# Hidden activations of a squared-ReLU MLP go through DRAM: the MLP in two phases, five of eight down groups by seven block products, the embedding projection between the phases

## The chip, the cores and the metric

The kernel runs on one core of one Trainium2 chip. A core has TensorE for matmuls (PE in the rows; its weight loads are PEld), VectorE (DVE), ScalarE (ACT) and GpSimd (POOL), and SyncE (SP), which here only issues DMAs; GpSimd issues DMAs as well. Operands lie in the on-chip buffer of 128 partitions, sums of matmuls in PSUM. The metric is the time of one execution on the device, in microseconds (us), as the median of the runs shown.

## The reference, cut to what matters

One decoder layer on 512 tokens with a model width of 2048, all in fp32. A gated linear attention comes first; the change does not touch it. Then:

```python
h = h + mix
h = h + square(relu(rmsnorm(h, norm_mlp) @ w_up)) @ w_down   # 2048 -> 8192 -> 2048
gate = sigmoid(rmsnorm(h, norm_ple) @ w_ple_gate)            # 2048 -> 2048
h = h + gate * (p @ w_ple_proj)                              # p: 512 x 256
return rmsnorm(h, norm_final)
```

## The kernel before, in words

**Products.** Each fp32 product is made of three matmuls in a faster 32-bit format (fp32r): both factors are split into a high and a low part, and hi·hi, hi·lo and lo·hi are added up in PSUM (mm3, L140 to L142). The weights are split on the way in by load_w (L126 to L132): SyncE's queue loads a tile `raw`, ScalarE casts it to `whi`, VectorE subtracts to get `wlo`. The pools have 3 buffers for raw, 4 for whi and 4 for wlo.

**Up products.** The hidden width of 8192 is made in 32 groups of 256 columns (up_group). A group walks in 4 chunks of 512 rows over the model width. Each chunk is cut into two-by-two blocks and multiplied by seven block products in place of eight (Winograd's form): sums of weight blocks T on VectorE (L783 to L786), casts (L793), low parts (L794), and 2 x 7 x 3 = 42 matmuls of 256 columns (L800 to L802). The operands on the token side, sums and differences of the blocks of the normalised h, are made once and stay (XS, XA). At the end of a group VectorE combines the seven sums (L808 to L814), applies ReLU and the rest of the norm's scale r2 (L816), ScalarE squares (L818), and the result is split into Sh and Sl (L821, L822).

**Down products.** The hidden values of two groups are one slice of 512. For each of 16 slices, 8 groups of 256 output columns are made plainly: 4 x 2 x 3 = 24 matmuls of 512 columns (down_group). The residual h passes through DRAM: GpSimd's queue loads two row blocks (L850), VectorE adds the sum of the slice (L859), GpSimd's queue stores them (L865). Only the last slice keeps h on the chip and makes the operands U of the gate from it (gain_split).

**Order.** The program is written so that up chunks of slice c alternate with down groups of slice c-1 (the loop at the end of the MLP); a scheduler then orders each engine's instructions, which run strictly in that order on their engine. The buffers in the pools set how far an engine can be ahead of TensorE.

**After the MLP.** p is transposed and split (PT), and for each of five groups of output columns the gate's product runs (ps_g), then for each of 4 blocks of tokens the embedding's projection (embed, ps_ple), the transposes of h (ps_h), and finish, which joins them.

## Time and profile before

| what | value |
|---|---|
| runs shown | 2389.72, 2767.68, 2387.84 us; median 2389.72 |
| profiled execution | 2387.21 us, its span 2385.4 us |
| mean granted TensorE clock | 0.997 |
| TensorE busy | 2366.7 us, 99% |
| VectorE busy | 1550.7 us, 65% |
| ScalarE busy | 868.2 us, 36% |
| GpSimd busy | 223.0 us, 9% |
| DMA | 382.85 MB, mean 160 GB/s |

Busy time counts the time in which an engine works on an instruction. Matmuls overlap each other, so the mean duration of one is longer than its share of the time; what a matmul costs is read from start to start. The granted clock is given as a share of TensorE's full 2.4 GHz.

### The profile page before, as it was taken

To read this page: it belongs to the slowest core of one execution; us is meant where nothing else is said; L and a number is where in the kernel's file an instruction comes from. 1 tells how busy PE (TensorE), PEld (TensorE's weight loads), DVE (VectorE), ACT (ScalarE), POOL (GpSimd) and SP (SyncE) were. 2 spreads that over 40 slices of the span, in tenths; PEclk is the share of its full clock that TensorE was granted. 3 is DMA by queue.
4 is the path that set the end of the run, shared out by engine and by line. 5 is a ranking of instruction groups with operands and counts; after the bars stand their busy time and mean duration, and the time that the engine had idled before them with its cause. 6 is when DMAs were issued, how large, how long until landed. Compare 5 with 4: busy or idle time off the path is not lost.

```text
span 2385.4 us, 33414 instructions
## 1 busy us (share of the span) xinstructions
PE 2366.7 (99%) x13360; PEld 2077.6 (87%) x13360; DVE 1550.7 (65%) x2457; ACT 868.2 (36%) x1287; POOL 223.0 (9%) x326
## 2 busy tenths in 40 slices
...
GB/s 256 102 84 102 89 80 106 80 97 85 106 168 150 125 140 201 198 193 206 206 204 194 200 202 202 203 201 199 202 195 204 203 204 200 200 267 123 84 80 80
DMA packets 257804, 382.85 MB, mean 160 GB/s; under 512 B 14324, under 2 KB 203440, under 8 KB 257648
## 3 DMA queue, kind: packets, MB, share of 16 engines
...
HBM read 302.02 MB, written 78.64 MB: 160 GB/s over the span
## 4 chain that ended last, share of the span: by engine, by line
PE 99%; DVE 0%; DMA 0%; issue 0%; ACT 0%; SPq 0%; ACTq 0%
PE ps_dn L140 10%; PE ps_dn L141 10%; PE ps_dn L142 10%; PE ps_up L800 9%; PE ps_up L802 9%; PE ps_up L801 9%; PE ps_g L142 2%; PE ps_g L141 2%; PE ps_v L140 2%; PE ps_g L140 2%; PE ps_wo L140 2%; PE ps_wo L141 2%; PE ps_og L142 2%; PE ps_v L142 2%; PE ps_v L141 2%; PE ps_og L141 2%
## 5 line engine op out<-in xcount | busy, mean ns | idle before, releaser
L140 PE MATMUL ps_dn<-Sh,whi_dn 128*128 128x512 f32 x1024 | 399.5, 390 | 0.0
L141 PE MATMUL ps_dn<-Sl,whi_dn 128*128 128x512 f32 x1024 | 399.5, 390 | 0.0
L142 PE MATMUL ps_dn<-Sh,wlo_dn 128*128 128x512 f32 x1024 | 398.4, 389 | 0.0
L793 ACT CAST whi_up<-raw_up 128x384 fp32r<-128x384 f32 x256 | 131.6, 514 | 443.9 <-PE ps_up L801 232.0
L800 PE MATMUL ps_up<-XS,whi_up 128*128 128x256 f32 x1024 | 290.1, 284 | 0.6 <-ACT whi_up L793 0.6
L801 PE MATMUL ps_up<-XS,whi_up 128*128 128x256 f32 x1024 | 289.4, 283 | 0.0
L802 PE MATMUL ps_up<-XS,wlo_up 128*128 128x256 f32 x1024 | 288.7, 283 | 0.0
L859 DVE TENSOR_TENSOR h<-h,ps_dn 128x512 f32<-128x512 f32 x256 | 172.0, 685 | 117.6 <-PE ps_dn L142 117.4
L130 ACT CAST whi_dn<-raw_dn 128x1024 fp32r<-128x1024 f32 x128 | 134.7, 1053 | 277.6 <-PE ps_dn L141 140.1
L142 PEld LDWEIGHTS ps_dn<-Sh,wlo_dn 128*128 128x128 f32 x1024 | 192.3, 188 | 40.6
L140 PEld LDWEIGHTS ps_dn<-Sh,whi_dn 128*128 128x128 f32 x1024 | 192.6, 188 | 37.6
L141 PEld LDWEIGHTS ps_dn<-Sl,whi_dn 128*128 128x128 f32 x1024 | 192.6, 188 | 36.6
L794 DVE TENSOR_TENSOR wlo_up<-raw_up,whi_up 128x384 fp32r<-128x384 f32 x256 | 141.7, 554 | 125.3 <-ACT whi_up L793 124.9
L801 PE MATMUL ps_up<-XA,whi_up 128*128 128x256 f32 x768 | 217.2, 283 | 0.0
L802 PE MATMUL ps_up<-XA,wlo_up 128*128 128x256 f32 x768 | 217.2, 283 | 0.0
L800 PE MATMUL ps_up<-XA,whi_up 128*128 128x256 f32 x768 | 216.9, 282 | 0.0
L132 DVE TENSOR_TENSOR wlo_dn<-raw_dn,whi_dn 128x1024 fp32r<-128x1024 f32 x128 | 156.8, 1225 | 67.3 <-ACT whi_dn L130 65.0
L800 PEld LDWEIGHTS ps_up<-XS,whi_up 128*128 128x128 f32 x1024 | 196.4, 192 | 1.7 <-ACT whi_up L793 1.4
L801 PEld LDWEIGHTS ps_up<-XS,whi_up 128*128 128x128 f32 x1024 | 196.5, 192 | 0.2 <-issue 0.2
L802 PEld LDWEIGHTS ps_up<-XS,wlo_up 128*128 128x128 f32 x1024 | 195.9, 192 | 0.1
L794 DVE TENSOR_TENSOR wlo_up<-T,whi_up 128x512 fp32r<-128x512 f32 x256 | 175.8, 689 | 10.6 <-ACT whi_up L793 10.6
L793 ACT CAST whi_up<-T 128x512 fp32r<-128x512 f32 x256 | 156.7, 615 | 46.4 <-DVE T L786 46.4
(302 smaller groups left out, 4781.4 us busy)
## 6 DMA issues: line engine op xcount, KB each, us to landing
h<-h_d POOLq DMA_DIRECT2D x128, 512.0 KB, 4.2
raw_up<-in_w_up SPq DMA_DIRECT2D x128, 512.0 KB, 4.3
raw_dn<-in_w_down SPq DMA_DIRECT2D x128, 512.0 KB, 4.5
h_d<-h POOLq DMA_DIRECT2D x120, 512.0 KB, 3.5
raw_v<-in_gla_w_in SPq DMA_DIRECT2D x32, 512.0 KB, 3.8
raw_og<-in_gla_w_in SPq DMA_DIRECT2D x32, 512.0 KB, 3.8
raw_wo<-in_gla_w_out SPq DMA_DIRECT2D x32, 512.0 KB, 3.6
raw_wg<-in_w_ple_gate SPq DMA_DIRECT2D x32, 512.0 KB, 3.6
```

What stands on the lines that cost most here:

```text
L130: nc.scalar.copy(hi, raw)
L132: nc.vector.tensor_tensor(out=lo, in0=raw, in1=hi.bitcast(F32), op=ALU.subtract)
L140: nc.tensor.matmul(ps, lhsT=wa[0], rhs=wb[0], start=first, stop=False)
L141: nc.tensor.matmul(ps, lhsT=wa[0], rhs=wb[1], start=False, stop=False)
L142: nc.tensor.matmul(ps, lhsT=wa[1], rhs=wb[0], start=False, stop=last)
L793: nc.scalar.copy(hi[:, o:o + n, :], src)
L794: nc.vector.tensor_tensor(out=lo[:, o:o + n, :], in0=src, in1=hi[:, o:o + n, :].bitcast(F32), op=ALU.subtract)
L800: nc.tensor.matmul(dst, lhsT=hi[:, wb, :], rhs=xh, start=kp == 0 and half == 0, stop=False)
L801: nc.tensor.matmul(dst, lhsT=hi[:, wb, :], rhs=xl, start=False, stop=False)
L802: nc.tensor.matmul(dst, lhsT=lo[:, wb, :], rhs=xh, start=False, stop=kp == NKP - 1 and (b == 3 or half == 1))
L859: nc.vector.tensor_tensor(out=hs[:, i, :], in0=hs[:, i, :], in1=ps[i], op=ALU.add)
```

## The change

The MLP runs in two phases. In the first all 32 up groups run, one behind the other; the hidden values z are no longer multiplied by r2 and split but stored to DRAM (z_d). In the second the 16 chunks of the hidden width are taken in five slices of 4, 3, 3, 3 and 3 chunks. For each slice all 8 output groups are made; groups 0, 3 and 7 plainly, the groups 1, 2, 4, 5 and 6 by seven block products with the same functions (chunk_sums, chunk, combine) as the up groups. The operands of a chunk are rebuilt from z_d by hidden_operands (Zh, Zl, Zdh, Zdl: eight slots of 34 per chunk). The missing scale is put on the residual: times g2 when the first slice reads it, times f2 when the last slice stores it. h is loaded and stored per slice and group, also at the last, and the gate's phase loads it again (residual). The sums of weight blocks are now made inside the raw tile, which has grown to 8 KB per partition; raw keeps 3 buffers, whi and wlo 4, and the tiles for loads (z, h and the like) 2 in place of 3. The embedding's projection runs between the phases: its weights in four tiles of 512 columns, its result through ScalarE into raw buffers and to DRAM (pp_d), to be loaded again in the gate's phase. The gate's scale r3 is made behind the gate's first group, and the gate's temporaries have two buffers, not six. The diff, cut to its core:

```diff
@@ load_w and pools
-        raw = wpool.tile(shape, F32, tag="raw", name=f"raw_{name}", bufs=3)
+    def wtile(shape, tag, name, dtype=F32):
+        return wpool.tile(shape, dtype, tag=tag, name=name, bufs={"raw": 3, "whi": 4, "wlo": 4, "ld": 2}[tag])
...
+    def chunk_sums(w, k4, g, name):
+        raw = wtile([P, 2, 8, P], "raw", f"raw_{name}")
...
+        nc.sync.dma_start(rows[:, :, 0, :], w_rows(w, 4 * k4, 4, 256 * g, 256))
+        tc.keep_in_program_order(nc.vector.tensor_tensor(
+            out=raw[:, :, 2:4, :], in0=raw[:, :, 1:5:3, :], in1=raw[:, :, 0:1, :].broadcast_to([P, 2, 2, P]),
+            op=ALU.add))
+        nc.vector.tensor_tensor(out=raw[:, :, 6, :], in0=raw[:, :, 2, :], in1=raw[:, :, 4, :], op=ALU.add)
+        nc.vector.tensor_tensor(out=raw[:, :, 7, :], in0=raw[:, :, 6, :], in1=raw[:, :, 5, :], op=ALU.add)
+    def chunk(ps, raw, k4, xops, first, last, name):
+        for q_ in range(2):
...
+            nc.scalar.copy(hi[:, 1:8, :], raw[:, q_, 1:8, :])
...
+                out=lo[:, 1:8, :], in0=raw[:, q_, 1:8, :], in1=hi[:, 1:8, :].bitcast(F32), op=ALU.subtract)
...
-        nc.vector.scalar_tensor_tensor(
-            out=z, in0=z, scalar=0.0, in1=r2.unsqueeze(1).broadcast_to([P, 2, T]), op0=ALU.max, op1=ALU.mult)
+    def hidden(g, ps):
+        z = combine(ps, f"up{g}")
+        nc.scalar.activation(out=z, in_=z, func=AF.Relu)
         nc.scalar.activation(out=z, in_=z, func=AF.Square)
...
+            nc.gpsimd.dma_start(z_d[g, :, f, :], z[:, 1 - f, :])
+    def residual_in(s_, g):
+        hs = load([P, 2, T], f"h_{s_}_{g}")
+        nc.gpsimd.dma_start(hs, h_d[g])
+        if s_ == 0:
+            nc.vector.tensor_tensor(out=hs, in0=hs, in1=g2.unsqueeze(1).broadcast_to([P, 2, T]), op=ALU.mult)
...
+    def add_slice(s_, g, ps):
+        z = combine(ps, f"dn{s_}_{g}")
+        hs = residual_in(s_, g)
+        for f in range(2):
+            nc.vector.tensor_tensor(out=hs[:, f, :], in0=hs[:, f, :], in1=z[:, 1 - f, :], op=ALU.add)
+        residual_out(s_, g, hs)
+    def hidden_operands(kp, u, d):
...
+        nc.scalar.copy(uh, ub)
+        nc.vector.tensor_tensor(out=d[:, 0:2, :], in0=ub[:, 0:2, :], in1=ub[:, 1:4:2, :], op=ALU.subtract)
+        nc.vector.tensor_tensor(out=d[:, 2, :], in0=ub[:, 0, :], in1=d[:, 1, :], op=ALU.subtract)
+        nc.vector.tensor_tensor(out=d[:, 3, :], in0=ub[:, 2, :], in1=d[:, 2, :], op=ALU.subtract)
+        nc.scalar.copy(dh, d)
+        nc.vector.tensor_tensor(out=ul, in0=ub, in1=uh.bitcast(F32), op=ALU.subtract)
+        nc.vector.tensor_tensor(out=dl, in0=d, in1=dh.bitcast(F32), op=ALU.subtract)
...
+    def project_embedding(gi):
+        hi, lo = load_w(w_rows(w_pp, 0, 2, 512 * gi, 512), [P, 2, 512], f"wp{gi}")
+        for t2 in range(NTT // 2):
+            o = wtile([P, 2, 512], "raw", f"pp_{gi}_{t2}")
...
+                nc.scalar.copy(o[:, t, :], ps)
+            nc.scalar.dma_start(
+                pp_d[2 * t2:2 * t2 + 2, :, 512 * gi:512 * gi + 512].rearrange("t p c -> p t c"), o)
...
+            if s_ == 0 and g == 0 and first:
+                for i in range(4):
+                    build_to(i // 2 + 1)
+                    project_embedding(i)
+            if g == 0:
+                build_to(k4 + 1)
...
+            if g == 2 and last and 8 * (SLICES[s_] + 1) <= 34:
+                build_to(end + 1)
...
+    def residual(kp):
+        h1[kp] = slot([P, 2, T], f"hf_{kp}")
+        nc.gpsimd.dma_start(h1[kp], h_d[kp])
```

What the change does to the engines' order, at three places. First TensorE at the start of a down group; before, the first of the 24 matmuls of group 0 of slice 14 (Sh and Sl are the hidden values' parts):

```order
L140 MATMUL ps_dn14_0_0_17824<-Sh_28_17254,whi_dn14_0_17830 128x512
L141 MATMUL ps_dn14_0_0_17824<-Sl_28_17255,whi_dn14_0_17830 128x512
L142 MATMUL ps_dn14_0_0_17824<-Sh_28_17254,wlo_dn14_0_17832 128x512
L140 MATMUL ps_dn14_0_1_17825<-Sh_28_17254,whi_dn14_0_17830 128x512
L141 MATMUL ps_dn14_0_1_17825<-Sl_28_17255,whi_dn14_0_17830 128x512
L142 MATMUL ps_dn14_0_1_17825<-Sh_28_17254,wlo_dn14_0_17832 128x512
```

Now, the first of the 42 of a chunk of group 1 in the second slice (Zh and Zl are parts of the hidden values, Zdh and Zdl of their block differences):

```order
L819 MATMUL ps_d1_1_0_15425<-Zh_8_15236,whi_d1_1_4_0_15429 128x256
L821 MATMUL ps_d1_1_0_15425<-Zl_8_15237,whi_d1_1_4_0_15429 128x256
L822 MATMUL ps_d1_1_0_15425<-Zh_8_15236,wlo_d1_1_4_0_15431 128x256
L819 MATMUL ps_d1_1_0_15425<-Zdh_8_15238,whi_d1_1_4_0_15429 128x256
L821 MATMUL ps_d1_1_0_15425<-Zdl_8_15239,whi_d1_1_4_0_15429 128x256
L822 MATMUL ps_d1_1_0_15425<-Zdh_8_15238,wlo_d1_1_4_0_15431 128x256
L819 MATMUL ps_d1_1_1_15426<-Zdh_8_15238,whi_d1_1_4_0_15429 128x256
L821 MATMUL ps_d1_1_1_15426<-Zdl_8_15239,whi_d1_1_4_0_15429 128x256
```

The matmuls have half the columns, and each accumulates into half a bank, with another weight block each time.

Second, VectorE where the embedding's weights are split. Before, this stands in the gate's phase, behind the MLP (wpl are the low parts of the embedding's weights, wlo_wg those of the gate's, y, u and r3 the gate's scale):

```order
L198 SCALAR_TENSOR_TENSOR y2_ple_18917<-u1_ple_18914,y1_ple_18912 128x4
L908 TENSOR_TENSOR PT_0_18932<-ps_pT0_18927,PT_0_18932 128x512
L195 TENSOR_TENSOR u2_ple_18919<-y2_ple_18917 128x4
L908 TENSOR_TENSOR PT_1_18940<-ps_pT1_18935,PT_1_18940 128x512
L196 SCALAR_TENSOR_TENSOR u2_ple_18919<-ms_ple_18903,u2_ple_18919 128x4
L198 SCALAR_TENSOR_TENSOR y3_ple_18922<-u2_ple_18919,y2_ple_18917 128x4
L896 COPY r3_18897<-y3_ple_18922 128x4
L926 TENSOR_TENSOR wpl0_18960<-raw_wp0_18956,wph0_18958 128x1024
L132 TENSOR_TENSOR wlo_wg0_5_19120<-raw_wg0_5_19116,whi_wg0_5_19118 128x1024
L132 TENSOR_TENSOR wlo_wg0_6_19150<-raw_wg0_6_19146,whi_wg0_6_19148 128x1024
```

Now, between the phases (wlo_wp2 and wlo_wp3 belong to the third and fourth tile of the embedding's weights, zd, Zl and Zdl to the operands of the second phase, h_0_0 and h_0_1 are residuals of the first slice that are rescaled, wlo_d0_0_0 is the first down weight of the phase):

```order
L141 TENSOR_TENSOR wlo_wp2_13523<-raw_wp2_13519,whi_wp2_13521 128x1024
L877 TENSOR_TENSOR Zdl_6_13745<-zd_6_13741,Zdh_6_13744 128x1024
L872 TENSOR_TENSOR zd_7_13755<-z_7_13753 128x512
L873 TENSOR_TENSOR zd_7_13755<-z_7_13753,zd_7_13755 128x256
L874 TENSOR_TENSOR zd_7_13755<-z_7_13753,zd_7_13755 128x256
L849 TENSOR_TENSOR h_0_0_13911<-h_0_0_13911,g2_5804 128x1024
L876 TENSOR_TENSOR Zl_7_13757<-z_7_13753,Zh_7_13756 128x1024
L877 TENSOR_TENSOR Zdl_7_13759<-zd_7_13755,Zdh_7_13758 128x1024
L849 TENSOR_TENSOR h_0_1_14148<-h_0_1_14148,g2_5804 128x1024
L141 TENSOR_TENSOR wlo_wp3_13565<-raw_wp3_13561,whi_wp3_13563 128x1024
L141 TENSOR_TENSOR wlo_d0_0_0_13609<-raw_d0_0_0_13605,whi_d0_0_0_13607 128x1024
L141 TENSOR_TENSOR wlo_d0_0_1_13639<-raw_d0_0_1_13635,whi_d0_0_1_13637 128x1024
```

The two last weight tiles of the projection stand between and behind the building of Z6 and Z7 and the two rescalings, and the first weights of the second phase stand behind them.

Third, VectorE within the MLP. Before, up chunks and down groups in turn (T are sums of weight blocks, h_12_4 a residual):

```order
L783 TENSOR_TENSOR T27_3_16745<-raw_up27_3_16743 128x2x256
L785 TENSOR_TENSOR T27_3_16745<-T27_3_16745,raw_up27_3_16743 128x2x128
L786 TENSOR_TENSOR T27_3_16745<-T27_3_16745,raw_up27_3_16743 128x2x128
L132 TENSOR_TENSOR wlo_dn12_5_16714<-raw_dn12_5_16710,whi_dn12_5_16712 128x1024
L859 TENSOR_TENSOR h_12_4_16611<-h_12_4_16611,ps_dn12_4_0_16609 128x512
L859 TENSOR_TENSOR h_12_4_16611<-h_12_4_16611,ps_dn12_4_1_16610 128x512
L794 TENSOR_TENSOR wlo_up27_6_16750<-raw_up27_3_16743,whi_up27_6_16749 128x384
L794 TENSOR_TENSOR wlo_up27_6_16750<-T27_3_16745,whi_up27_6_16749 128x512
L794 TENSOR_TENSOR wlo_up27_7_16777<-raw_up27_3_16743,whi_up27_7_16776 128x384
L794 TENSOR_TENSOR wlo_up27_7_16777<-T27_3_16745,whi_up27_7_16776 128x512
L132 TENSOR_TENSOR wlo_dn12_6_16811<-raw_dn12_6_16807,whi_dn12_6_16809 128x1024
```

Now, inside the second phase, group 2 of the first slice, with the combination of group 1 (e_dn0_1) in it:

```order
L801 TENSOR_TENSOR raw_dn2_1_14027<-raw_dn2_1_14027 128x2x256
L804 TENSOR_TENSOR raw_dn2_1_14027<-raw_dn2_1_14027 128x2x128
L805 TENSOR_TENSOR raw_dn2_1_14027<-raw_dn2_1_14027 128x2x128
L813 TENSOR_TENSOR wlo_d0_2_0_0_14038<-raw_dn2_0_13972,whi_d0_2_0_0_14036 128x896
L813 TENSOR_TENSOR wlo_d0_2_0_1_14063<-raw_dn2_0_13972,whi_d0_2_0_1_14061 128x896
L801 TENSOR_TENSOR raw_dn2_2_14086<-raw_dn2_2_14086 128x2x256
L804 TENSOR_TENSOR raw_dn2_2_14086<-raw_dn2_2_14086 128x2x128
L805 TENSOR_TENSOR raw_dn2_2_14086<-raw_dn2_2_14086 128x2x128
L813 TENSOR_TENSOR wlo_d0_2_1_0_14093<-raw_dn2_1_14027,whi_d0_2_1_0_14091 128x896
L830 TENSOR_TENSOR e_dn0_1_14141<-ps_d0_1_0_13802,e_dn0_1_14141 128x256
L831 TENSOR_TENSOR e_dn0_1_14141<-e_dn0_1_14141,ps_d0_1_1_13803 128x256
L832 TENSOR_TENSOR e_dn0_1_14141<-ps_d0_1_1_13803,e_dn0_1_14141 128x2x256
```

Down weights now have sums, subtractions of 896 elements and a combination in PSUM's half banks, as up weights have; the plain subtraction of 1024 elements and the add from PSUM are left in groups 0, 3 and 7.

## Rows read from the trace of the kernel before

**Rows 1.** The page: span, busy times by engine, and the chain that ended last.

```profile
span 2385.4 us, 33414 instructions
...
PE 2366.7 (99%) x13360; PEld 2077.6 (87%) x13360; DVE 1550.7 (65%) x2457; ACT 868.2 (36%) x1287; POOL 223.0 (9%) x326
...
PE 99%; DVE 0%; DMA 0%; issue 0%; ACT 0%; SPq 0%; ACTq 0%
```

**Rows 2.** Busy time by stage: window, length, engines (instructions), granted clock, DMA share, GB/s.

```profile
818.00:869.00 51.00, 50.35 (x406) 49.10 (x405) 46.34 (x97) 25.89 (x47) 1.44 (x2) 1.00 0.33 104
...
1000.00:1500.00 500.00, 500.00 (x3144) 454.52 (x3143) 358.37 (x559) 177.01 (x274) 68.67 (x96) 1.00 0.63 200
```

**Rows 3.** TensorE in order of time: start us, duration us, line, operation.

```profile
2106.01 0.28 PE L800 MATMUL ps_up<-XA,whi_up 128*128 128x256 f32 x1
...
2111.05 0.40 PE L140 MATMUL ps_dn<-Sh,whi_dn 128*128 128x512 f32 x1
...
2165.47 0.39 PE L140 MATMUL ps_g<-whi_wg,U_norm_ple 128*128 128x512 f32 x1
```

**Rows 4.** Embedding matmuls by form: busy us, mean ns | idle before (one of three lines).

```profile
L140 PE MATMUL ps_ple<-wph,PT 128*128 128x512 f32 x24 | 10.1, 419 | 0.0
...
L140 PE MATMUL ps_ple<-wph,PT 128*128 128x256 f32 x16 | 4.8, 302 | 0.1
```

**Rows 5.** VectorE by form, 800 to 2150 us.

```profile
L794 DVE TENSOR_TENSOR wlo_up<-T,whi_up 128x512 fp32r<-128x512 f32 x256 | 175.8, 689 | 10.6 <-ACT whi_up L793 10.6
L859 DVE TENSOR_TENSOR h<-h,ps_dn 128x512 f32<-128x512 f32 x250 | 167.9, 685 | 117.5 <-PE ps_dn L142 117.4
L132 DVE TENSOR_TENSOR wlo_dn<-raw_dn,whi_dn 128x1024 fp32r<-128x1024 f32 x128 | 156.8, 1225 | 67.3 <-ACT whi_dn L130 65.0
...
L783 DVE TENSOR_TENSOR T<-raw_up 128x512 f32<-128x512 f32 x127 | 87.9, 692 | 16.1 <-DMA raw_up<-in_w_up 12.3
L785 DVE TENSOR_TENSOR T<-T,raw_up 128x256 f32<-128x256 f32 x127 | 53.9, 425 | 4.0
...
L811 DVE TENSOR_TENSOR e<-ps_up,e 128x512 f32<-128x512 f32 x32 | 22.1, 690 | 1.0
...
L809 DVE TENSOR_TENSOR e<-ps_up,e 128x256 f32<-128x256 f32 x32 | 13.3, 416 | 0.0
```

**Rows 6.** VectorE in order of time, 848 to 855 us.

```profile
848.90 1.23 DVE L822 TENSOR_TENSOR Sl<-e,Sh 128x1024 fp32r<-128x1024 f32 x1 [0.26 <-ACT Sh L821]
850.04 0.68 DVE L794 TENSOR_TENSOR wlo_up<-T,whi_up 128x512 fp32r<-128x512 f32 x1
850.65 0.55 DVE L794 TENSOR_TENSOR wlo_up<-raw_up,whi_up 128x384 fp32r<-128x384 f32 x1
...
853.75 1.29 DVE L794 TENSOR_TENSOR wlo_up<-T,whi_up 128x512 fp32r<-128x512 f32 x2 [0.69 <-ACT whi_up L793]
```

**Rows 7.** The page: DMA issues, KB each, us from issue to landing.

```profile
h<-h_d POOLq DMA_DIRECT2D x128, 512.0 KB, 4.2
...
raw_dn<-in_w_down SPq DMA_DIRECT2D x128, 512.0 KB, 4.5
h_d<-h POOLq DMA_DIRECT2D x120, 512.0 KB, 3.5
```

**Rows 8.** ScalarE's casts, from the page's groups.

```profile
L793 ACT CAST whi_up<-raw_up 128x384 fp32r<-128x384 f32 x256 | 131.6, 514 | 443.9 <-PE ps_up L801 232.0
...
L130 ACT CAST whi_dn<-raw_dn 128x1024 fp32r<-128x1024 f32 x128 | 134.7, 1053 | 277.6 <-PE ps_dn L141 140.1
```

**Rows 9.** Busy time by stage at the start; the columns of Rows 2.

```profile
5.00:10.00 5.00, 3.32 (x13) 2.14 (x13) 3.08 (x5) 3.24 (x4) 0.55 (x1) 0.79 1.05 352
10.00:15.00 5.00, 4.32 (x14) 3.06 (x14) 2.78 (x5) 2.66 (x10) 0.54 (x1) 0.53 1.12 343
15.00:20.00 5.00, 5.00 (x25) 4.11 (x24) 3.11 (x5) 1.75 (x3) 0.00 (x0) 1.00 0.89 272
```

414 lines of the change are left out of this document (232 added, 182 removed).

## The prediction, made before the changed kernel ran

> **What bounds the kernel now.** I read the page first, then the table by stage, then the order in time, then the groups by form. The page's first part and its chain of waits [rows 1] say one thing: TensorE is busy 99% of the span, and the chain that ends last is TensorE for 99%. The table by stage [rows 2] shows that this holds stage by stage and is no average: in 1000 to 1500 us, with up and down products interleaved, TensorE is full, VectorE at 358 of 500 us, ScalarE at 177. So time can be gained only by shorter TensorE work, and lost only where TensorE, now never late, begins to wait. The row to keep in mind is 818 to 869 us: there only up products ran, with the building of the operands beside them, VectorE was at 46.34 of 51 us (91%), and TensorE lost 0.65 us. VectorE can be this full without being the bound.
>
> **TensorE's own work.** The order in time [rows 3] gives prices from start to start, which are right for pipelined matmuls. From 2106.01 to 2111.05 run the 42 matmuls of 256 columns of one up chunk: 5.04 us, 0.120 each. From 2111.05 to 2165.47 run the last ten down groups, 240 matmuls of 512 columns: 54.42 us, so 5.44 us for the 24 of a group. The change replaces 24 by 42 in five of eight groups for all 16 chunks: 80 x (5.44 - 5.04) = -32.2 us. Three groups keep 24. Up products are as before. The embedding projection had 72 matmuls of 512 and 48 of 256 columns [rows 4], 72 x 0.227 + 48 x 0.120 = 22.1 us; now it has 96 of 512, 21.8 us: -0.3. One more broadcast of a scale over the partitions costs some +0.9 (an estimate: two wide matmuls at twice the row's price). Without any wait the end would be 2387.2 - 31.6 = 2355.6 us, 1.3% under the profiled execution's 2387.21. That is the floor, so faster by over 2% needs something that is not in the trace.
>
> **Phase 1.** VectorE's prices are in [rows 5]. Of one up chunk: sums 0.692 + 2 x 0.425 = 1.54; two subtractions of 896 elements, which the trace doesn't have; between 128x512 (0.689) and 128x1024 (1.225) the line gives 1.09 each. Combining a group: three of 256 and two of 512 elements, 2.63. A group: 4 x 3.72 + 2.63 = 17.5 us beside 20.2 of TensorE, 87%, less than in the stage that lost almost nothing. I take 0. By the loss of that stage, 0.65 per 51 us, it would be 8 over 645 us.
>
> **The boundary between the phases is the main term.** The order of VectorE's instructions shows that after the combination of up30 come the rest of up31, the building of all hidden operands Z0 to Z7, two rescalings of the residual, and between them the four wlo_wp that the projection needs, the last of them behind Z7 and behind h_0_1. Summed from [rows 5] up to wlo_wp3: combinations of up30 and up31 5.3; five wlo_up 5.45; two sums of chunks 3.1; two PT 1.4; four wlo_wp 4.9; sixteen Zl and Zdl of 1024 elements 19.6; seven zd 7 x 1.53 = 10.7; two rescalings 2.4; together 52.8 us. Independent neighbours on VectorE overlap a little [rows 6]: 0.68 us long, the next starts 0.61 later; 1.23, and 1.14 later. With 0.08 off for each of 66 instructions it is 47.5. TensorE has in the same stretch up31 (20.2), the transposes of p (some 0.9) and three of four projection groups (16.3): 37.4 us, then it needs wlo_wp3. It waits 10.1 to 15.4 us in all, in pieces ahead of up31's last chunks and of wp1, wp2, wp3. On top comes a wait of VectorE: h_0_1's load waits for a buffer that Zl_7 frees, takes 4.2 us [rows 7], and only Zdl_7 (1.2) lies beside it: 3.0. Then the first down weights: their buffer is raw_wp3's, free when wlo_wp3 is made; load 4.5 [rows 7], cast 1.05 [rows 8], subtraction 1.2, together 6.8 against 5.44 of projection: 1.4. That is 14.5 to 19.8. Each Zl and Zdl also waits for its cast on ScalarE, of which some isn't covered. I take 20; the ends are 10 (close spacing, the load of h_0_1 early) and 28 (one cast of 1.05 exposed for each of eight builds on top).
>
> Of the overlap the Trainium skill, page "VectorE: DVE Perf Modes", section "The DRAIN you can't avoid", says that the next operation does not start until the pipe is empty. By that the durations would simply add and the boundary would be at its upper figure; [rows 6] show starts 0.07 to 0.09 before the end of the one ahead, so here I go between the two.
>
> **Phase 2.** TensorE has 80 x 5.04 + 48 x 5.44 = 664 us. VectorE: 80 x 3.72 + 48 x 1.225 + 25 x 2.63 + 40 x 1.37 (residual adds, 0.685 each) + 12 builds of Z behind the boundary counted as 24 half chunks of 3.98 + 14 further rescalings of 1.22 = 298 + 59 + 66 + 55 + 96 + 17 = 591 us, 89%. In a seven-product group of three chunks it is 3 x 3.72 + 2.63 + 1.37 = 15.2 beside 15.12, so there VectorE falls behind or just holds and lives on the lead that the plain groups give (5.05 beside 16.3). At the change of slices the next Z operands can only be made when the last group has released slots: 8 us of VectorE per chunk beside 5.44. The lead covers nearly all of it. The row of 818 to 869 us prices such a stage at 0.65 per 51 us, 8.5 over the phase; I take 4, with 0 and 9 as ends. Residual loads and stores are 4.2 and 3.5 us [rows 7] and have a whole group of 15 us; the reload for the gate has 38 us from hf_7's load to its use. For the gate's later scale (r3 is now made behind the first gate group) and two temporaries in place of six: 2, between 0 and 4.
>
> **Sum.** 2387.2 - 31.6 + 20 + 4 + 2 = 2381.6. The profiled execution lies 2.5 below the median of the runs shown (2389.72), so I say **2382**: 0.3% below, no change that can be told. What a measurement of this kernel tells from no change is taken as 2%, 48 us: faster is below 2342, slower above 2437.
>
> **Rival 1: the boundary is nearly hidden.** VectorE's pieces come early enough (the casts are made ahead, neighbours overlap) and phase 2 has no waits: 2355.6 + 10 + 0 to 2 = about 2366. For it: the 91% of [rows 2]. Against it: the order puts 47 us of VectorE into 37 of TensorE, which no lead can cover. Chance 0.22, for anything from 2356 to 2373.
>
> **Rival 2: the holes bring TensorE's clock down.** The trace has one hole early, between 5 and 10 us; there the granted clock is 0.79 and in the next 5 us 0.53 [rows 9], the level of 1.2 GHz, and 1.00 again after that. In the boundary the holes are 2 to 7 us each, with 5.44 us of matmuls between. If these run at half speed, a group takes 10.9; ahead of wp2 and wp3 much of this only fills time that is waited for, behind wlo_wp3 it is on the path. One group late costs 5.4, three cost 16: 2387 to 2398, say 2391. The Trainium skill, "TensorE: Matmul & The Clock Gate", section "HAM oscillation — how this bites in real kernels", describes just this, bursts of matmuls that start at the low clock after each wait. It is for that rival; [rows 9] agree for one hole. Chance 0.20.
>
> **Rival 3, slower: VectorE becomes the bound through phase 2.** Here it must not be the sum of its work but its waits: each subtraction waits for the cast of its own half chunk, because ScalarE can cast only when TensorE frees one of four buffers. In the trace of before ScalarE waits 232 us for exactly that [rows 8], and the last of [rows 6] shows VectorE waiting 0.69 for the cast. A cast of 896 elements is 0.95 (between 0.51 for 384 and 1.05 for 1024, [rows 8]). Exposed twice in 80 chunks and once (1.05) in 48: 152 + 50 = 202 us, against 664 - 591 = 73 of room: +129, 2507. It decides from 73 / 128 = 0.57 us of waiting per chunk, and passes 2437 at about 1.0. Against it: four buffers are two chunks, so the cast can be made 5 us before use; the stage at 91% ran with the same four. Chance 0.05 for above 2437, and 0.05 for 2400 to 2437.
>
> **Numbers.** Forecast as worked out, 2373 to 2392: 0.47; rival 1 0.22; rival 2 with its tail to 2400 0.20; 2400 to 2437 0.05; above 2437 0.05; below 2342, by nothing that I can name, 0.01. The range from **2362 to 2402** leaves out the lower half of rival 1 and what lies above. Faster 0.02, same 0.93, slower 0.05.
>
> **What would show it.** TensorE's busy time by starts in phase 2 should give 0.120 and 0.227 per matmul, and the idle time ahead of ps_ple and the first ps_d0_0 some 20 us, released by VectorE's wlo_wp and wlo_d0 (and raw_d0's load). If the idle time there is under 8, my sum of VectorE's order is wrong; if the granted clock there falls to 0.5 and the matmuls are 0.43 apart, rival 2 holds. If TensorE's idle time is spread over phase 2 with wlo_d as the releaser, it is rival 3. The prediction is wrong in its base if the matmuls of 256 columns in the down products cost more than 0.120 each.

## The result, and the profile after

The changed kernel takes **2422.9 us** (median of four runs, 2420.5 to 2424.4) against 2388.8 of the kernel before: ratio 1.0144, 95% interval 1.0124 to 1.0164. One of the four runs before, of 2767.7 us, was in a slower state and is left out of the ratio. The kernel is slower by 1.4%: that is clear of the interval, within the 2% that the forecast took as no change, and outside the range of 2362 to 2402. The forecast said 2382.

The page after, answering to [rows 1]: span, busy times, chain that ended last.

```profile
span 2422.2 us, 36477 instructions
...
PE 2361.6 (97%) x14778; PEld 2136.3 (88%) x14778; DVE 1690.2 (70%) x2579; ACT 977.5 (40%) x1216; POOL 152.5 (6%) x282
...
PE 78%; issue 8%; DVE 5%; DMA 4%; ACT 1%; POOL 0%; ACTq 0%; DVEq 0%; POOLq 0%
```

TensorE was the chain for 99% of the span; now it is for 78%. It waits, and the table by stage says where (columns of [rows 2], whose two windows come first):

```profile
818.00:869.00 51.00, 44.27 (x244) 38.78 (x243) 37.23 (x75) 17.30 (x25) 1.89 (x3) 0.90 0.30 94
1000.00:1500.00 500.00, 498.95 (x4158) 498.63 (x4157) 406.76 (x617) 243.03 (x276) 28.17 (x52) 1.00 0.43 131
840.00:860.00 20.00, 13.27 (x82) 12.67 (x81) 18.35 (x34) 9.33 (x13) 1.33 (x2) 0.74 0.33 106
1500.00:1520.00 20.00, 15.06 (x55) 11.28 (x53) 16.53 (x23) 14.55 (x19) 3.24 (x6) 0.83 0.72 238
1520.00:1540.00 20.00, 13.29 (x36) 9.60 (x37) 12.63 (x15) 8.31 (x11) 1.06 (x2) 0.76 0.57 194
```

Phase 1 (second row) is full, and VectorE at 407 of 500 us does no harm there. The loss lies in short places, in each of which the granted clock (the first figure behind the engines' busy times) is below 1.00 too. The list of TensorE's waits names them: instruction that waited, releaser, us in all, times, longest (eight of its lines). Such waits are called holes below.

```profile
PE ps_xT L249 <- DMA x<-in_x: 8.0, 3, 4.1
PE ps_ple L149 <- ACT whi_wp L139: 7.6, 3, 2.8
PE ps_wo L149 <- ACT whi_wo L139: 5.0, 2, 4.1
PE ps_d L150 <- DVE Zl L876: 5.0, 4, 2.2
PE ps_ple L150 <- DVE wlo_wp L141: 4.0, 3, 1.6
PE ps_up L819 <- ACT whi_up L811: 3.7, 2, 2.6
PE ps_ts_mlp L215 <- DVE acc L683: 3.6, 1, 3.6
PE ps_d L149 <- ACT whi_d L139: 2.2, 1, 2.2
```

What each place costs, its holes and what follows them, is read from TensorE's first instructions of each stage, start to start. **The ledger**, in us, from the two profiled runs:

| stretch | before | after | more |
|---|---|---|---|
| start to the first V product (ps_v) | 75.3 | 86.1 | 10.8 |
| attention up to the output projection | 566.5 | 566.5 | 0 |
| output projection (ps_wo, first to last) | 176.7 | 187.3 | 10.7 |
| from there to the first ps_up | 0.2 | 8.0 | 7.8 |
| phase 1, to the first ps_ple | up and down together 1346.8 | 652.7 | |
| boundary, to the first ps_d | | 44.9 | |
| phase 2, to the first ps_g | | 679.0 | |
| gate and end (before with the embedding projection) | 219.9 | 197.7 | -22.2 |

Up, projection and down are now 1376.6 us against 1346.8 + 22.1 before: **29.2 us are lost ahead of the MLP**, 7.7 more in it, where the prediction had 7.6 less (-31.6 + 20 + 4).

Three causes ahead of the MLP are seen in the order of time of the engine that is late; the first three experiments test them. SyncE at the start (x loads of L244, weight loads of L137; a group's length is that of all its issues):

```profile
1.65 10.23 SPq L137 DMA_DIRECT2D raw_qk<-in_gla_w_in  x5
11.93 0.50 SPq L244 DMA_DIRECT2D x<-in_x  x1
...
33.22 14.87 SPq L137 DMA_DIRECT2D raw_v<-in_gla_w_in  x3
48.14 2.01 SPq L244 DMA_DIRECT2D x<-in_x  x3
```

The x loads, which now take a slot, are issued behind weight loads that wait for one of three raw buffers: the second x only at 11.93 us, the last three at 48.14. In the kernel before, the second and third went out at 2.74:

```profile
2.74 1.14 SPq L235 DMA_DIRECT2D x<-in_x  x2
```

ScalarE in the output projection:

```profile
787.94 0.63 ACT L682 ACTIVATE sq_mlp<-xres 128x512 f32<-128x512 f32 x1 [14.19 <-issue]
789.83 0.63 ACT L682 ACTIVATE sq_mlp<-xres 128x512 f32<-128x512 f32 x1 [1.26 <-DVE acc L683]
790.50 0.40 ACT L722 CAST XA<-u_late 128x256 fp32r<-128x256 f32 x1
790.81 1.99 ACT L139 CAST whi_wo<-raw_wo 128x1024 fp32r<-128x1024 f32 x2
```

u_late holds one of the three raw buffers that the weights need, and the cast of the next weight stands behind ScalarE's squares and its cast from u_late: TensorE waits 4.1 us for it. In the kernel before, the cast came ahead of the squares:

```profile
775.14 1.05 ACT L130 CAST whi_wo<-raw_wo 128x1024 fp32r<-128x1024 f32 x1 [4.39 <-PE ps_wo L141]
776.10 0.62 ACT L678 ACTIVATE sq_mlp<-xres 128x512 f32<-128x512 f32 x1
```

VectorE at the entry of phase 1:

```profile
842.94 0.69 DVE L683 TENSOR_TENSOR acc<-acc,sq_mlp 128x512 f32<-128x512 f32 x1
...
844.82 0.68 DVE L801 TENSOR_TENSOR raw_up<-raw_up 128x512 f32<-128x512 f32 x1
...
846.21 0.42 DVE L805 TENSOR_TENSOR raw_up<-raw_up 128x256 f32<-128x256 f32 x1
```

The sums of the first weight chunk, pinned in program order, come behind the last residual's work, and on TensorE the token sums (which wait for acc) stand ahead of the first up product: 3.6 + 2.6 us of waiting in the 8.0, and 0.5 just behind.

### The profile page after: what moved, and what is told of

Same layout as the page of the kernel before. It is cut to its first block, busy times and chain, and to the rows that moved or that the text cites. A ratio compares the mean times of both kernels' runs of the same rounds, so it can differ in the third digit from the quotient of the medians.

```text
span 2422.2 us, 36477 instructions
## 1 busy us (share of the span) xinstructions
PE 2361.6 (97%) x14778; PEld 2136.3 (88%) x14778; DVE 1690.2 (70%) x2579; ACT 977.5 (40%) x1216; POOL 152.5 (6%) x282
## 4 chain that ended last, share of the span: by engine, by line
PE 78%; issue 8%; DVE 5%; DMA 4%; ACT 1%; POOL 0%; ACTq 0%; DVEq 0%; POOLq 0%
PE ps_up L822 9%; PE ps_up L819 9%; PE ps_up L821 9%; PE ps_d L821 5%; PE ps_d L819 5%; PE ps_d L822 4%; DMA z<-z_d 3%; PE ps_wo L151 2%; PE ps_v L149 2%; PE ps_wo L149 2%; PE ps_v L150 2%; PE ps_og L150 2%; PE ps_v L151 2%; PE ps_og L149 2%; PE ps_og L151 2%
## 5 line engine op out<-in xcount | busy, mean ns | idle before, releaser
L811 ACT CAST whi_up<-raw_up 128x896 fp32r<-128x896 f32 x256 | 239.8, 940 | 317.5 <-PE ps_up L821 309.5
L813 DVE TENSOR_TENSOR wlo_up<-raw_up,whi_up 128x896 fp32r<-128x896 f32 x256 | 277.7, 1087 | 92.9 <-ACT whi_up L811 92.9
L813 DVE TENSOR_TENSOR wlo_d<-raw_dn,whi_d 128x896 fp32r<-128x896 f32 x160 | 172.9, 1087 | 35.6 <-ACT whi_d L811 34.8
L821 PE MATMUL ps_d<-Zdl,whi_d 128*128 128x256 f32 x640 | 181.1, 283 | 0.0
L819 PE MATMUL ps_d<-Zdh,whi_d 128*128 128x256 f32 x640 | 181.1, 283 | 0.0
L822 PE MATMUL ps_d<-Zdh,wlo_d 128*128 128x256 f32 x640 | 181.1, 283 | 0.0
L150 PE MATMUL ps_d<-Zl,whi_d 128*128 128x512 f32 x384 | 151.9, 396 | 5.0 <-DVE Zl L876 5.0
L149 PE MATMUL ps_d<-Zh,whi_d 128*128 128x512 f32 x384 | 151.7, 395 | 3.9 <-ACT whi_d L139 2.2
L151 PE MATMUL ps_d<-Zh,wlo_d 128*128 128x512 f32 x384 | 151.5, 394 | 0.5 <-DVE wlo_d L141 0.5
L819 PEld LDWEIGHTS ps_up<-XA,whi_up 128*128 128x128 f32 x768 | 147.9, 193 | 4.2 <-ACT whi_up L811 3.9
L821 PEld LDWEIGHTS ps_up<-XA,whi_up 128*128 128x128 f32 x768 | 148.0, 193 | 0.2 <-issue 0.2
```

The lines of the kernel that those rows point to most:

```text
L149: nc.tensor.matmul(ps, lhsT=wa[0], rhs=wb[0], start=first, stop=False)
L150: nc.tensor.matmul(ps, lhsT=wa[0], rhs=wb[1], start=False, stop=False)
L151: nc.tensor.matmul(ps, lhsT=wa[1], rhs=wb[0], start=False, stop=last)
L811: nc.scalar.copy(hi[:, 1:8, :], raw[:, q_, 1:8, :])
L813: nc.vector.tensor_tensor(out=lo[:, 1:8, :], in0=raw[:, q_, 1:8, :], in1=hi[:, 1:8, :].bitcast(F32), op=ALU.subtract)
L819: nc.tensor.matmul(dst, lhsT=hi[:, wb, :], rhs=xh, start=first and q_ == 0 and half == 0, stop=False)
```

## The experiments

All times are medians, each against runs of the kernel before on the same chip (medians 2386.5 to 2387.8 us; 2388.8 for the changed kernel). The columns behind the ratio are the stretches of the ledger, from one profiled run each. That run lies within 3.1 us of its kernel's median, but 6.8 above it in b4_ld3 and 6.9 below it in b3_fill.

| kernel | us | ratio to before, interval | start | ps_wo | entry | phase 1 | boundary | phase 2 |
|---|---|---|---|---|---|---|---|---|
| changed | 2422.9 | 1.0144 (1.0124 to 1.0164) | 86.1 | 187.3 | 8.0 | 652.7 | 44.9 | 679.0 |
| e1_x_ld | 2412.7 | 1.0103 (1.0088 to 1.0118) | 78.1 | 187.2 | 8.3 | 652.2 | 44.8 | 677.4 |
| e2_u_late | 2408.3 | 1.0085 (1.0070 to 1.0100) | 85.7 | 178.4 | 8.0 | 652.7 | 45.0 | 674.4 |
| e3_entry | 2404.8 | 1.0073 (1.0058 to 1.0088) | 86.5 | 186.4 | 0.2 | 651.0 | 45.6 | 670.7 |
| e4_boundary | 2404.2 | 1.0069 (1.0052 to 1.0086) | 84.7 | 187.2 | 8.0 | 652.6 | 34.5 | 671.8 |
| b1_all | 2380.9 | 0.9974 (0.9964 to 0.9984) | 78.8 | 179.3 | 0.2 | 651.0 | 25.3 | 679.3 |
| b1_plain8 | 2404.5 | 1.0073 (1.0056 to 1.0090) | 77.8 | 179.9 | 0.2 | 651.0 | 24.5 | 705.9 |
| b1_plain2 | 2383.4 | 0.9987 (0.9976 to 0.9998) | 78.8 | 179.3 | 0.2 | 651.0 | 25.7 | 682.4 |
| b1_slices | 2392.9 | 1.0024 (1.0012 to 1.0036) | 77.8 | 179.8 | 0.2 | 651.0 | 25.4 | 691.8 |
| b2_pp_slots | 2384.3 | 0.9987 (0.9978 to 0.9996) | 78.0 | 179.3 | 0.2 | 649.7 | 23.6 | 688.6 |
| b2_early | 2387.0 | 1.0000 (0.9990 to 1.0009) | 79.0 | 179.7 | 0.2 | 649.7 | 23.6 | 688.8 |
| b2_plain2 | 2383.5 | 0.9981 (0.9972 to 0.9991) | 77.5 | 179.6 | 0.2 | 649.7 | 23.6 | 686.5 |
| after_fill | 2408.7 | 1.0091 (1.0074 to 1.0108) | 82.9 | 187.4 | 8.0 | 652.8 | 40.7 | 668.7 |
| b1_idle | 2399.0 | 1.0049 (1.0034 to 1.0064) | 79.0 | 180.1 | 0.2 | 669.0 | 25.4 | 681.3 |
| b3_ul | 2387.2 | 0.9999 (0.9989 to 1.0009) | 76.8 | 179.4 | 0.2 | 651.1 | 25.6 | 685.4 |
| b3_fill | 2389.1 | 1.0003 (0.9993 to 1.0012) | 77.3 | 179.0 | 0.2 | 651.1 | 25.1 | 683.6 |
| c_fill | 2396.9 | 1.0040 (1.0025 to 1.0055) | 77.3 | 179.0 | 0.2 | 651.0 | 41.9 | 679.7 |
| b4_ld3 | 2388.3 | 1.0005 (0.9994 to 1.0015) | 79.9 | 181.9 | 0.2 | 655.3 | 25.6 | 681.6 |
| b4_ld3e | 2381.3 | 0.9975 (0.9964 to 0.9986) | 76.8 | 181.8 | 0.2 | 654.9 | 25.6 | 670.4 |

**One place each.** e1_x_ld, the x and gated loads from a pool of two again:

```
-        xc[cc] = slot([P, NTT, 256], f"x_{cc}")
+        xc[cc] = load([P, NTT, 256], f"x_{cc}")
```

> The changed kernel, but the loads of x and of the gated values take their tiles from the pool of two load buffers, as they did before (there with three), not from the 34 slots. My theory: in the changed kernel the first TensorE holes (3.39 us at 19.47 and 4.08 us at 55.93, both released by a load of x) come from SyncE's order, in which loads of x stand behind weight loads that wait for a buffer; the first ps_v starts at 86.06 in place of 75.31 us. Then this run gives back 9 to 11 us and ps_v starts at 75 to 77: about 2412 to 2414 us. Rival: the holes come from the DMA engines, which are full there (DMA share 1.05), whatever the order: under 3 us, 2420 to 2423.

Measured: 10.3 us less, 8.0 of it at the start, as the theory has it. Some 3 us at the start stay open: 78.1 against 75.3. e2_u_late, the late residuals out of the weights' pool:

```
-                late["s"] = wtile([P, 2, 2, T], "raw", "u_late")
+                late["fg"] = mpool.tile([P, 2, T], F32, tag="fg", name="u_5")
...
-                late["u"] = late["s"][:, kp - 5, :, :]
+                late["u"] = late["fg"] if kp == 5 else load([P, 2, T], "u_6")
```

> The changed kernel, but the two late normalised blocks (u_5 and u_6) no longer lie in one of the three raw buffers of the weights: u_5 takes the place of the two scales, u_6 a load buffer. My theory: with a raw buffer gone, the cast of the next output weight stands behind the whole evacuation of block 5 on ScalarE; that is the hole of 4.09 us at 791.90 with 0.99 behind it, and the half clock after it; ps_wo lasts 187.3 in place of 176.7 us. Then this run gives back 9 to 11 us: 2412 to 2414. Rival: the evacuation chain on VectorE and ScalarE is late by itself, since the operands are made in another order: 0 to 2 us.

14.6 less, more than said: 8.9 in the output projection, where ScalarE's cast now stands ahead of the squares again, and 4.6 in phase 2, in which nothing was edited. e3_entry, the token sums two groups later, and the chunk sums of the first up group not pinned:

```
-            if g == 0 and k4 == 2:
+            if g == 2 and k4 == 2:
                 rest_of_scale()
...
-        tc.keep_in_program_order(nc.vector.tensor_tensor(
+        pin = (lambda i: i) if name.startswith("up0_") else tc.keep_in_program_order
+        pin(nc.vector.tensor_tensor(
```

> The changed kernel, but the norm's scale (its sums over tokens wait for the squares of the last block) is made two up groups later, and the block sums of the first up group are not held in program order on VectorE. My theory: the 8.0 us between the last ps_wo and the first ps_up (before: 0.2) are TensorE standing behind the token sums (3.64) and behind block sums that VectorE may only make after the operands of the last block (2.60 for the cast); half clock follows until 856. Then this run gives back 8 to 12 us: 2411 to 2415. Rival: VectorE has too much to do there (operands of blocks 5 to 7), so the wait only moves to the next operands: 2 to 4 us, 2419 to 2421.

18.1 less, more than said: the entry is gone (8.0 to 0.2), and phase 2, again unedited, is 8.3 shorter (the section on the prediction comes back to that). e4_boundary, the projections ahead of the building of the operands, each group's result in one raw tile:

```
                 for i in range(4):
-                    build_to(i // 2 + 1)
                     project_embedding(i)
```

> The changed kernel, but the four projections of the embedding come first and all building of the second phase's operands after them, and the result of a projection lies in one raw buffer in place of two. My theory: the 23.2 us that the boundary costs over its matmuls are VectorE's order (wlo_wp1 to wlo_wp3 behind Z3, Z5 and Z7) and the half clock after each hole; the same VectorE work, spread under the projections and the first down group, fits: 15 to 21 us come back, 2402 to 2408. Rival: VectorE's work is the same, so the holes only move to the first down group: 2 to 6 us, 2417 to 2421.

18.7 less, as said: 10.4 in the boundary, 7.2 in phase 2. What is left of the boundary is ScalarE, whose cast of the next weight stands behind its copies of the results. ScalarE in order of time, in e4_boundary:

```profile
1503.28 0.59 ACT L940 COPY pp<-ps_ple 128x512 f32<-128x512 f32 x1 [0.77 <-PE ps_ple L151]
...
1505.19 1.06 ACT L139 CAST whi_wp<-raw_wp 128x1024 fp32r<-128x1024 f32 x1
```

**All together.** b1_all loads and splits all four embedding weights before the first projection besides:

```
+                wps = [embedding_weights(i) for i in range(4)]
                 for i in range(4):
-                    build_to(i // 2 + 1)
-                    project_embedding(i)
+                    project_embedding(i, wps[i])
```

> The first three repairs (the x and gated loads from the pool of two, the late residuals out of the pool of three, the entry of phase 1) and the fourth in a sharper form: all four embedding weights are split before the first copy of a projection. Theory (the loss is a sum of independent orders in four places, each found by name): gains of 10.3, 14.6, 18.1 and 18.7 us from 2422.9 give 2361; 5 us of phase 2's recovery may be counted twice, the sharper fourth may give 5 to 10 more: 2353 to 2368, faster than the kernel before by about 1%. Rival (a hole closed moves the wait elsewhere; the new pools bind anyhow): 2375 to 2392.

2380.9: 42 us of the 61.7, faster than the kernel before by 0.26%. Everything ahead of phase 2 came back about as in the single repairs, and the boundary by more (25.3 of 44.9), so the ledger holds there; phase 2 did not stay short (679.3). Waits of TensorE in b1_all, the two largest:

```profile
PE ps_d L150 <- DVE Zl L877: 7.3, 5, 2.8
PE ps_d L149 <- ACT whi_d L139: 3.4, 1, 3.4
```

My reading, which no run isolates: the projections had covered the building of the first slice's operands; with TensorE there sooner, part of the wait has moved behind them. The total lies in the rival's range.

**What the down products give.** b1_plain8:

```
-PLAIN = (0, 3, 7)
+PLAIN = (0, 1, 2, 3, 4, 5, 6, 7)
```

> The same kernel as b1_all, all eight down groups as plain products. Theory (the five groups of seven products give what TensorE's count says, since nothing of the loss lay there): 32 us more than b1_all, some 2388 to 2400, all of it in phase 2. Rival (VectorE's extra work in phase 2 takes a good part back): less than 20 us more than b1_all.

23.6 more, 26.6 of it in phase 2: between the theory's 32 and the rival's 20. The count of TensorE's work holds; some 5.5 us of it go back in phase 2, where the plain version has holes of 4.1 us in all against 8.3 (VectorE works 344 us in its phase 2, against 569). b1_plain2, group 3 by seven products too (PLAIN = (0, 7)):

> The same kernel as b1_all, with group 3 by seven products too, so two plain groups are left of three. Theory (TensorE bounds phase 2, VectorE has room: 79% busy in its first stretch): 16 chunks less by 0.40 us each, 6 us under b1_all. Rival (without the plain group between them, VectorE falls behind over four groups in a row): 0 to 30 us over b1_all.

The rival: 2.4 more in place of 6 less; its holes in phase 2 are 15.0 us against 8.3. b1_slices, SLICES = (3, 3, 3, 3, 4):

> The same kernel as b1_all, with the slice of four chunks last in place of first, so that the operands of the second slice are built ahead as those of the later ones are. Theory (the holes of 0.6 and 2.2 us behind TensorE's first slice come from operands that are not built ahead, and half clock follows them): 3 to 7 us under b1_all. Rival (the hole moves to the later, longer slice or its clock cost is not there): within 2 us of b1_all.

The theory is wrong by sign, and the rival too: 12 us more. The second slice's operands still come late (holes of 2.1, 2.7 and 2.2 us there) and VectorE's wlo_d is late in the first slice too. Building one chunk ahead was not enough to remove these holes.

**What sets the pace of the operands.** b2_pp_slots puts the projections' results into slots (o = slot([P, 2, 512], ...)) in place of raw buffers:

> b1_all with the projections' results in the pool of 34 slots in place of the weights' pool of three. In b1_all TensorE waited 3.4 and 0.5 us ahead of its first down product for a weight whose load stood behind these results, and 0.7 and 2.8 us in the chunk after it for operands that stood behind that weight on VectorE. Theory (one late load stands behind all four): 7.4 us of holes go, with the half clock behind them 8 to 12 us: 2369 to 2373. Rival (the operands are late by themselves: their reloads and one difference tile set the pace): only the first 3.9 us go, 2375 to 2379.

Theory and rival are both wrong, 3.4 us more: the wait for the weight went, boundary 23.6, but phase 2 is 9.3 longer, with new holes in its first 55 us, of up to 3.9 us. b2_early adds build_to(end + 2) in the first chunk of group 7:

> As b2_pp_slots, and the operands of each next slice are built one chunk earlier, beside group 7 of the slice before. Theory (the holes of 0.5 to 2.2 us at the starts of the later slices, 4.4 us in b1_all, come from building two chunks of operands within one plain group, where the reload takes 4 us and the building some 4 us for half a chunk): they go, with what the clock adds 5 to 9 us under b2_pp_slots, 2361 to 2367. Rival (VectorE cannot take it beside group 7 either, the hole moves ahead into that group): within 2 us of b2_pp_slots or above.

The rival came true: 2.7 us more, and holes of 16.1 us in phase 2 against 14.9. b2_plain2 is b2_early with PLAIN = (0, 7):

> As b2_early, with group 3 by seven products too. Theory (b1_plain2 lost its 6 us to the same late operands, 6.5 us more of holes than b1_all, not to VectorE's sum of work): 3 to 7 us under b2_early, 2356 to 2364. Rival (with six groups of eight VectorE has no plain group left to catch up in, and the holes stay): 0 to 10 us over b2_early.

3.5 less, as the theory has it for the difference; its total (2356 to 2364) and its ground are wrong, since b2_early had not removed the late operands, and the holes are 18.2 us here. b3_ul moves VectorE's Zl ahead of the differences:

```
         nc.scalar.copy(uh, ub)
+        nc.vector.tensor_tensor(out=ul, in0=ub, in1=uh.bitcast(F32), op=ALU.subtract)
...
-        nc.vector.tensor_tensor(out=ul, in0=ub, in1=uh.bitcast(F32), op=ALU.subtract)
```

> b1_all with VectorE's remainder of the hidden pair (Zl), which the first, plain group needs, ahead of the four instructions for the differences, which only the second group needs; 1.5 us of work on VectorE then stand behind it instead of ahead. Theory (order): the holes on Zl of 2.8, 2.2, 0.9 and 0.8 us lose up to 1.5 us each, 3 to 5 us in all, with their half clock 4 to 9 us: 2372 to 2377. Rival (the sum of VectorE's work and the reloads set it, the next operand comes late instead): within 2 us of b1_all.

Both miss: 6 us more. The waits on Zl fell to 3.8 us, but waits on ScalarE's cast Zh took their place. TensorE's waits in b3_ul:

```profile
PE ps_d L149 <- ACT Zh L872: 7.1, 3, 3.4
PE ps_d L150 <- DVE Zl L873: 3.8, 4, 1.3
```

A residual's store and the reload of one hidden pair behind it, as GpSimd issues them:

```profile
1807.89 0.54 POOL L856 DMA_DIRECT2D h_d<-h  x1 [3.64 <-DVE h L893]
1811.20 0.53 POOL L901 DMA_DIRECT2D z<-z_d  x1 [2.77 <-DVE raw_dn L806]
```

And ScalarE's cast, which starts when it has landed:

```profile
1814.86 1.04 ACT L872 CAST Zh<-z 128x1024 fp32r<-128x1024 f32 x1 [0.97 <-DMA z<-z_d]
```

The store had landed 2.9 us after its issue, 0.4 us before the reload went out; the releaser that the row names is inferred. So VectorE's order alone is not it. A likelier cause: each pair of hidden rows must be reloaded into one of two buffers, which the residual tiles use too. b4_ld3 and b4_ld3e test that:

```
-bufs={"raw": 3, "whi": 4, "wlo": 4, "ld": 2}[tag])
+bufs={"raw": 3, "whi": 4, "wlo": 3, "ld": 3}[tag])
```

> b1_all with three buffers in the pool of loads in place of two, and three for the weights' low parts in place of four. Theory (reload of a hidden pair, 4 us, and building, 4 us, take turns in two buffers that the residual tiles share, so two pairs take longer than the plain chunk of 5.5 us that needs them): the holes on Zl behind the slices' starts (2.8, 2.2, 0.9, 0.8 us) shrink by over half, phase 2 falls from 679 to 669 to 675, total 2371 to 2377; phase 1 stays at 651 if three low parts do. Rival (VectorE's own work in the plain group sets it): phase 2 within 2 us of 679, total 2379 to 2383. Other rival (three low parts bind everywhere): phase 1 over 655.

> b4_ld3 and the operands of each next slice built one chunk earlier, beside group 7. Theory (the earlier building was held by the same two buffers): the holes at the later slices' starts go altogether, 2 to 5 us under b4_ld3, 2367 to 2374. Rival (it only moves the holes into group 7 or to the next reload, as with two buffers): within 3 us of b4_ld3.

In both the waits on Zl and Zh behind the first slice are gone (from 4.4 us to none over 0.25). In b4_ld3 waits on VectorE's wlo_d, with one buffer fewer, take their place (8.0 us in 7), so that run alone could hide late operands behind them. b4_ld3e, with the earlier building that was worthless on two buffers, has holes of only 2.8 us in its phase 2 of 670.4, and that points to the two buffers. The exchange is paid for: phase 1, the output projection, and the gate with the end are 4, 2.5 and 4.6 us longer than in b1_all; phase 1 is over 655 in b4_ld3, as the other rival said. Both totals miss their theories (2388.3 for 2371 to 2377, 2381.3 for 2367 to 2374). TensorE's waits in b4_ld3e:

```profile
PE ps_d L149 <- ACT whi_d L139: 3.7, 1, 3.7
...
PE ps_d L823 <- DVE wlo_d L814: 1.7, 1, 1.7
```

The total of b4_ld3e is that of b1_all: bought with one buffer, paid with another.

**What a hole costs.** b1_idle is b1_all with three waits of TensorE put into the full phase 1, each for a chain of small copies on ScalarE:

```
+            if k4 == 1 and g in (4, 8, 12):
+                idle({4: 3, 8: 8, 12: 16}[g], g)
```

> b1_all with three holes put on purpose into phase 1, where TensorE is busy 20.00 of 20 us: in up groups 4, 8 and 12, after the second chunk, TensorE waits for a chain of 4, 9 and 17 small copies on ScalarE (0.29 us each: holes of some 1.3, 2.7 and 5 us, 9 us in all). Theory (a hole costs itself and a stretch of half clock behind it): beside the holes, 0 to 5 us each of half clock, the granted clock under 1.00 in these windows alone; b1_all + 9 + (3 to 12), 2393 to 2402. Rival (a hole costs itself alone, and the half clock has another cause): b1_all + 9 to 11, 2390 to 2392, clock 1.00.

18 us more, as the theory has it. The waits were 1.84, 3.49 and 6.12 us (the copies of a chain start 0.33 us apart, not 0.29), 11.5 in all. TensorE in order of time, behind the first and the third wait:

```profile
922.32 0.49 PE L978 MATMUL ps_idle<-ones,idle 128*128 128x128 f32 x2 [1.84 <-ACT idle L977]
...
923.58 0.42 PE L824 MATMUL ps_up<-XS,whi_up 128*128 128x256 f32 x1
923.80 0.42 PE L825 MATMUL ps_up<-XS,wlo_up 128*128 128x256 f32 x1
...
926.77 0.28 PE L824 MATMUL ps_up<-XA,whi_up 128*128 128x256 f32 x1
926.89 0.28 PE L825 MATMUL ps_up<-XA,wlo_up 128*128 128x256 f32 x1
...
1097.61 0.80 PE L978 MATMUL ps_idle<-ones,idle 128*128 128x128 f32 x2 [6.12 <-ACT idle L977]
...
1100.55 0.41 PE L825 MATMUL ps_up<-XS,wlo_up 128*128 128x256 f32 x1
```

From 923.4 to 926.6 us products of 256 columns start 0.213 apart, then 0.12 again. Much the same follows the second wait (to 1012.0) and the third (to 1100.8): 3.2 to 3.4 us behind the wait at the lower of the two levels, 1.2 GHz, which cost 1.2 to 1.5 us each, as much behind the shortest wait as behind the longest. With the chains' own small products (2.3 us) that is 11.5 + 3.9 + 2.3 = 17.7 of the 18.0. The Trainium skill, "TensorE: Matmul & The Clock Gate", section "HAM oscillation — how this bites in real kernels", describes bursts of matmuls that start at the low clock behind waits of 3 to 5 us each. The second and third wait, of 3.49 and 6.12 us, agree; the first, of 1.84 us, was enough as well, and the fall came 1.0 us behind its end. So a wait of 1.8 us costs 3.3 here, and one of 6.1 costs 7.4.

Not every hole brings the clock down, though. One of 2.22 us in phase 2 of the same run left it at 1.00 (1710 to 1720 us), as did one of 2.76 us in b1_all (1520 to 1540 us):

```profile
1710.23 0.50 PE L151 MATMUL ps_d<-Zl,whi_d 128*128 128x512 f32 x1 [2.22 <-DVE Zl L879]
```

The same hole of 2.16 us ahead of the first down product was followed by the lower level in the changed kernel and not in e3_entry. What decides it no run here settles.

after_fill adds products that nothing reads, in the holes of the changed kernel's boundary:

```
+        if gi:
+            fill(11, gi)
```

> The changed kernel itself, with products that nothing reads put on TensorE ahead of the embedding projections 1, 2 and 3 (11 each, 512 columns) and of the first down product (9), on operands that have long been there: 42 x 0.227 us = 9.5 us of work in the places where TensorE stood idle for 2.8, 2.6, 2.2 and 2.2 us. Nothing that was waited for comes earlier. Theory (of the 45.0 us from the first projection to the first down product 21.8 are work, 13.8 holes and 9.4 the half clock that follows the holes): the granted clock there rises from 0.83 and 0.76, and although 9.5 us of work are added the stretch falls to 36 to 42 us. Rival (the pace of VectorE, ScalarE and the reloads sets the stretch, and a faster TensorE only waits longer): 44 to 47 us. Other rival (the fill lands on half clock itself): 48 to 55 us.

**14.3 us less by adding work.** The boundary is 40.7 with 9.5 us more in it, the clock there 1.00 and 0.91 for 0.83 and 0.76; and phase 2, where nothing was edited, is 668.7 for 679.0: the theory's range. The two windows of the boundary in after_fill:

```profile
1500.00:1520.00 20.00, 17.20 (x72) 12.97 (x71) 18.33 (x25) 16.54 (x22) 3.11 (x6) 1.00 0.80 273
1520.00:1540.00 20.00, 16.94 (x65) 12.56 (x64) 8.96 (x10) 7.23 (x11) 0.66 (x2) 0.91 0.62 213
```

In the boundary holes and fill together are 15.3 us, against 13.8 of holes before, so nothing was won there but the clock: TensorE worked 15.8 us at 1.2 GHz in the changed kernel and 3.4 here. About 3 us of the 14.3 lie at the start, where the runs of the same instructions differ by as much (82.9 to 86.5). b3_fill, the same trick (14 products) ahead of b3_ul's first down product:

> b3_ul with 14 products that nothing reads (3.2 us at full clock) ahead of the first down product, where TensorE waits 3.4 us for a weight. Theory (half clock behind a hole): the chunk behind it runs at full clock, 2 to 5 us under b3_ul. Rival (the operands behind it come no earlier, so the time goes into their holes): within 1 us of b3_ul.

No gain (1.9 more, and the profiled runs 2.0 apart the other way): the fill took the hole's place, and phase 2 ends no earlier. c_fill, the first three repairs with after_fill's products and b3_ul's order:

> The changed kernel with the first three repairs alone, its boundary as it was (projections between the building), with the fill of after_fill and the order of b3_ul. Theory (each gain adds: 10 at the start, 9 in the output projection, 8 at the entry, 14 by the fill, 0 to 4 by the order, out of 2422.9): 2376 to 2384. Rival (fill and repairs win the same microseconds of phase 2): 2385 to 2392.

Rival missed by 5 us and theory by 13: boundary 41.9 and phase 2 679.7. The last projection waits 4.8 us for wlo_wp there. What became of after_fill's gain can't be told: c_fill also has b3_ul's order, which by itself had cost 6 us, and no run has the three repairs without the fill.

## Why the prediction was wrong

**The step that failed** is the one behind "Without any wait the end would be 2355.6": the base. It took all that stands ahead of the MLP as unchanged, and costed of the diff only what multiplies, adds and combines. The diff also moves x, gated and the late residuals between pools, cuts the pool of loads from three to two, and pins sums. Those stretches cost 10.8 + 10.7 + 7.8 = 29.2 (before rounding) of the 41 us by which the forecast was short (42 in the profiled run); e1, e2 and e3 take back 8.0, 8.9 and 7.8 of them in place. The rest is 10.7 more than its term in phase 2, 3 in the boundary and 2 in phase 1, less 2 in the gate. My own rule, that TensorE was never late and could only begin to wait, should have been put to each of those moves.

**TensorE's work: right.** The prices of [rows 3] hold in the new products. TensorE in order of time in the changed kernel, 42 products of 256 columns from 1601.09 to 1606.13, 5.04 us:

```profile
1601.09 0.28 PE L819 MATMUL ps_d<-Zdh,whi_d 128*128 128x256 f32 x1
...
1606.13 0.28 PE L819 MATMUL ps_d<-Zdh,whi_d 128*128 128x256 f32 x1
```

b1_plain8 gives 23.6 to 26.6 of the 32.2 in time; most of the rest goes back in phase 2's waits.

**Phase 1: right.** It takes 652.7 for 645.1 of up products, 7.6 more; up and down before took 1346.8 for 645.1 + 696.3 (128 x 5.44), 5.4 more. Of the 2.2 between them e3_entry takes back 1.7. The subtraction of 896 elements, bounded between two rows of [rows 5], is 1087 ns, the 1.09 that was taken.

**The boundary: right in place and nearly in size, but in part by luck.** 44.9 - 21.8 of projection = 23.1 against 20 (10 to 28). The last weight stands behind the reloaded residual, as was said, and VectorE waits 3.49 us for it against 3.0. VectorE in order of time, in the changed kernel:

```profile
1529.49 1.22 DVE L877 TENSOR_TENSOR Zdl<-zd,Zdh 128x1024 fp32r<-128x1024 f32 x1
1534.20 1.23 DVE L849 TENSOR_TENSOR h<-h,g 128x1024 f32<-128x1024 f32 x1 [3.49 <-DMA h<-h_d]
1535.34 1.22 DVE L141 TENSOR_TENSOR wlo_wp<-raw_wp,whi_wp 128x1024 fp32r<-128x1024 f32 x1
```

But it is 13.8 us of holes and 9.3 of other loss, most of it half clock (15.8 us of work at 1.2 GHz, of which nearly half is lost). So the size was right by two errors: **rival 2 came true inside it**, where I had it as an alternative, and the pure waiting was under 20. Nor was VectorE's sum the bound: VectorE is busy for 28.6 of the 44.9 us. Only 4.0 of the 13.8 us of holes end with its wlo_wp; 9.8 end with ScalarE's casts (whi_wp 7.6, whi_d 2.2), which stand behind its copies of the projections' results and its casts for the operands. VectorE itself waits 3.00 us for one of these:

```profile
1519.05 1.23 DVE L877 TENSOR_TENSOR Zdl<-zd,Zdh 128x1024 fp32r<-128x1024 f32 x1 [3.00 <-ACT Zdh L875]
```

The prediction had no copies on ScalarE in its sum; b1_all, where all four weights are split ahead of the first copy, has no hole on whi_wp or wlo_wp left. TensorE behind the last wait for wlo_wp, 512 columns 0.43 apart:

```profile
1538.35 0.63 PE L150 MATMUL ps_ple<-wlo_wp,PT 128*128 128x512 f32 x1
1538.78 0.63 PE L151 MATMUL ps_ple<-whi_wp,PT 128*128 128x512 f32 x1
```

**Phase 2: mis-sized**, 679.0 - 664.3 = 14.7 for a term of 4 (0 to 9). VectorE's work was priced about right (its instructions last 597 us in all, 591 said), but neighbours overlap, which the prediction took off at the boundary and not here, so it is busy for only 552. The loss came from elsewhere: 7.3 us of holes, 6.8 of them on Zl and Zh of the later slices, where b4_ld3 and b4_ld3e point to the two load buffers, and half clock behind some of them. These two make up the phase in the six kernels whose phase 2 was not edited; in us, from the traces:

| kernel | phase 2 | holes | TensorE's work at 1.2 GHz |
|---|---|---|---|
| changed | 679.0 | 7.3 | 10.2 |
| e1_x_ld | 677.4 | 6.3 | 10.2 |
| e2_u_late | 674.4 | 4.4 | 6.8 |
| e4_boundary | 671.8 | 4.2 | 3.3 |
| e3_entry | 670.7 | 4.6 | 0 |
| after_fill | 668.7 | 2.6 | 0 |

A product at 1.2 GHz takes 0.213 us in place of 0.120, or 0.43 in place of 0.227, so nearly half of the last column is lost. With 664.3 of work and the holes that leaves 2 to 3 us in each. So what moved by itself in e1 to e4 and after_fill is which holes open there and which of them the lower level follows; why that changes with edits elsewhere stays open.

**The gate: 0** in place of 2. **Rival 3** did not occur: phase 2's waits lie at the slices' starts and not at each wlo_d.

Where the expected gain went, then: TensorE saved its 32 us, and gave them and 37 more of span back as 29 ahead of the MLP, 23 at the boundary and 15 in phase 2. With the orders mended, 0.26% is what the change is worth (b1_all).
